# Weight parts interleaved column by column, and a distance table for one product, in a two-layer hybrid block on one core

## The chip, the core and the metric

The kernel runs on one core of one Trainium2 chip. The time is device microseconds of one execution. Three runs of the kernel before are shown, and one profiled execution, from which all rows come.

## The reference

The reference takes 256 tokens of width 1024, puts 16 learned tokens ahead of them, and applies two layers. A layer is a mixer and a feed-forward block, each behind a root-mean-square norm, and each added to its input. The mixer multiplies by one wide matrix and splits the result into the inputs of three branches (retention, a gated recurrence in chunks, differential attention) and three gates; each branch is multiplied by a matrix of its own, the gated sum by an output matrix. The feed-forward block is:

```python
u = jnp.where(valid[None, :, None], hn @ w_ffn_in, 0.0)
up = jnp.pad(u, ((0, 0), (CONV_W - 1, 0), (0, 0)))
c = conv_b + sum(conv_w[j] * up[:, j:j + l] for j in range(CONV_W))
gate, val = jnp.split(c, 2, axis=-1)
return (jax.nn.silu(gate) * val) @ w_ffn_out
```

A last norm ends it. Everything is float32. What matters here is that nearly all of the work is products of a long stream of weights with an activation `x` of at most 272 tokens.

## The kernel before

**Layout.** Features lie on the 128 partitions and tokens along the free axis, 272 of them (16 + 256). An activation of width 1024 is eight slices of 128 features, `x_k`, each 272 columns of 4 bytes. Tiles of four such slices stand next to each other, so a slice begins 1088 bytes after the one ahead of it: 64 bytes further on, counted modulo 256.

**Three products for one.** A float32 product is made of three products in a rounded float32 format (`fp32r` in the profile). Both sides are split into a high part and a low part: `hi` is the value rounded, `lo` is the rest. For each weight tile of 128x128 TensorE does high times high (L910), high weight times low `x` (L911) and low weight times high `x` (L912), all into one PSUM tile `main`. The weight tile is what is loaded into the array (LDWEIGHTS), `x` is what streams through it. Each of the three matmuls has a load of its own, which the trace shows in the lane PEld, beside the matmul that runs ahead of it.

**The stream of weights.** The weights are stored in the order of use, as 404 chunks of eight tiles (128x1024 float32, 512 KB). For every chunk SP issues the DMA to `wraw` (three buffers), ScalarE copies it with rounding to `whi` (four buffers), VectorE subtracts to give `wlo` (four buffers). Each of these is one instruction for a whole chunk, with very few exceptions; they read `wraw` without gaps and leave gaps in what they write. A product works through its tiles in the order `_turns` gives: a pair of output tiles f = 0, 1 for each input slice k.

**Where a tile lies in its chunk.** `_places` leaves gaps between the tiles, such that the tile for slice k starts at a fixed place modulo 256 bytes (`LINE`), which moves by 64 bytes from k to k + 1 as `x_k` does. The two numbers in `APART` set it, the first where 272 columns stream, the second in most of the second layer, where only 258 do (the streamed columns then start 14 columns, 56 bytes, later, `T0`). `BLOCK` makes up for `x` that lies in other buffers. With the addresses of the built program, a weight tile starts 48 bytes after the start of the columns that stream against it where 272 do, and 48 bytes ahead of it where 258 do, both modulo 256. The fourth pair of the second feed-forward product (`fo`, j = 3) has no wanted place in the first layer, and the whole last product has none in the second layer, where the chunk itself streams (512 columns) and the activations `ghi` and `glo` are loaded (L1513 to L1515).

**Order.** All instructions are recorded by `_Plan` and put into an order by its costs and due times; an engine then works in that order. A chunk's copy and subtraction are due 6 us (`LEAD`) ahead of its matmuls. A product's output is taken out of PSUM by VectorE or ScalarE (`evacuate`, `rotate`), and the branches' small products are spread among the large ones by hand-written marks in `ORDER`.

Of the kernel before, what the change touches and what calls it, by code (L numbers as in the profile page):

```python
# [11 lines left out]
F32 = mybir.dt.float32  # L12
F32R = mybir.dt.float32r
U8 = mybir.dt.uint8
AF = mybir.ActivationFunctionType
ALU = mybir.AluOpType
PSUM = bass.MemoryType.PSUM
ADD, SUB, MUL = ALU.add, ALU.subtract, ALU.mult

P = 128  # L20
DEPTH = 2
# [18 lines left out]
CHUNK_TILES = 8  # L40
# [52 lines left out]
def _turns(li):  # L93

    pairs = [x for x in ORDER if x[0][0] not in MARKS]
    if li == DEPTH - 1:
        pairs = [x for x in pairs if x[0] != "fo"]  # L100
    groups = [[x] for x in pairs]
    if li == 0:
        groups[:2] = [pairs[:2]]
    turned = [[pairs[pairs.index((name, 0)) + DEFER - 1]] for name in ("hq", "fi")]
    out = []
    for group in groups:
        if group == [("fo", 3)]:
            out.append([("fo", 3, k, f) for f in range(2) for k in range(FK)])
        else:
            nk = _ktiles(group[0][0])  # L110
            out.append([x + (k, f) for k in range(nk // 2) for x in group for f in range(2)])
            out[-1] += [x + (k, f) for x in group for k in range(nk // 2, nk) for f in range(2)]
            if group in turned:
                out[-1] = out[-1][nk:] + out[-1][:nk]
    if li == DEPTH - 1:
        out.append([("fo", j, k, f) for k in range(FK) for j in range(KD // 2) for f in range(2)])
    return out
# [2 lines left out]
STREAM = sum(2 * _ktiles(n) for n, _ in ORDER if n[0] not in MARKS)  # L120


LINE = 256
APART = (240, 200)
BLOCK = 64
ROOM = CHUNK_TILES * P + 2 * LINE // 4
T0 = META - 2
FULL = ("rk", "rv", "hf", "hi", "dk", "dv")

# [1 line left out]
def _places(depth=DEPTH):  # L131

    wants = []
    for li in range(depth):
        for name, j, k, _ in sum(_turns(li), []):
            if name == "fo" and (li == DEPTH - 1 or j == 3):
                wants.append(None)
                continue  # L140
            short = li == DEPTH - 1 and name not in FULL
            wants.append(APART[short] + BLOCK * (name[0] == "b" or name in ("wo", "fo")) + 64 * (k % 4))
    out = []
    for c in range(0, len(wants), CHUNK_TILES):
        at, places = 0, []
        for want in wants[c : c + CHUNK_TILES]:
            if want is not None:
                at += (want // 4 - at) % (LINE // 4)
            places.append(at)
            at += P  # L150
        assert at <= ROOM
        out.append(places)
    return out


def _runs(places):


    runs = []
    for i, at in enumerate(places):  # L160
        if runs and at == runs[-1][1] + runs[-1][2] * P:
            runs[-1][2] += 1
        else:
            runs.append([i, at, 1])
    out = []
    for i, at, n in runs:
        if out and out[-1][4] == n and (out[-1][3] == 1 or at == out[-1][1] + out[-1][2] * out[-1][3]):
            if out[-1][3] == 1:
                out[-1][2] = at - out[-1][1]
            out[-1][3] += 1  # L170
        else:
            out.append([i, at, 0, 1, n])
    return out
# [424 lines left out]
class _Weights:  # L598
# [3 lines left out]
    def __init__(self, plan, pool, w, act, dve, sp):  # L602
        self.plan, self.pool, self.w = plan, pool, w
        self.act, self.dve, self.sp = act, dve, sp
        self.used = 0
        self.places = _places()

    def part(self, t, at, step, runs, n):

        return bass.AP(t.tensor, t.offset + at, [list(t.ap[0]), [max(step, 1), runs], [1, n * P]])  # L610

    def next(self):
        c, i = divmod(self.used, CHUNK_TILES)
        self.used += 1
        if i == 0:
            due = self.plan.key
            room = [P, ROOM]
            raw = self.plan.tile(self.pool, [P, CHUNK_TILES * P], F32, "wraw", 3, f"wraw{c}")
            hi = self.plan.tile(self.pool, room, F32R, "whi", 4, f"whi{c}")
            lo = self.plan.tile(self.pool, room, F32R, "wlo", 4, f"wlo{c}")  # L620
            self.plan.key = due - LEAD
            pieces = 1 if c > 1 else 2
            for p in range(pieces):
                n = CHUNK_TILES // pieces
                cols = slice(p * n * P, (p + 1) * n * P)
                self.sp.dma_start(raw[:, cols], self.w[c][:, cols])
                for first, at, step, runs, each in _runs(self.places[c][p * n : (p + 1) * n]):
                    src = raw[:, (p * n + first) * P : (p * n + first + runs * each) * P].rearrange("p (r x) -> p r x", r=runs)
                    self.act.activation(self.part(hi, at, step, runs, each), src, AF.Copy)
                    self.dve.tensor_tensor(out=self.part(lo, at, step, runs, each), in0=src, in1=self.part(hi, at, step, runs, each).bitcast(F32), op=SUB)  # L630
            self.plan.key = due
            self.cut = hi, lo
        hi, lo = self.cut
        at = self.places[c][i]
        return hi[:, at : at + P], lo[:, at : at + P]

    def chunk(self):

        for _ in range(CHUNK_TILES):
            self.next()  # L640
        return self.cut


def build(tc, a, depth=DEPTH, probe=None):
# [1073 lines left out]
```

## Time and profile before

| | |
|---|---|
| median of 3 runs | 1304.37 us (1304.02 to 1306.12) |
| profiled execution, own time | 1304.55 us |
| span in its trace | 1302.8 us |
| TensorE busy | 1293.8 us, 99% of the span |
| VectorE busy | 990.1 us, 76% |
| ScalarE busy | 853.1 us, 65% |
| GpSimd busy | 85.0 us, 7% |
| DMA | 219.01 MB, mean 168 GB/s |
| granted TensorE clock | full in all 40 slices |

Busy time says that an engine has an instruction under way. Matmuls overlap in the array, so a matmul's own duration (285 ns or so) is not what it costs: the cost is the distance from its start to the next one's start. That is read from how many matmuls a stretch of time holds. In such a count the two records that only reach into the stretch at its ends are taken off.

### The profile page before, as it was taken

What the parts mean: (1) busy time and instruction counts of PE and PEld (TensorE: products, weight loads), DVE (VectorE), ACT (ScalarE), POOL (GpSimd) and SP (SyncE); (2) the same over time, 40 slices, a digit from 0 to 9 for tenths busy, and PEclk for the clock granted to TensorE, in tenths of its full rate; (3) what the DMA queues carried; (4) which work ended last, traced back from release to release, by engine and by line L of the source; (5) the groups of instructions that cost most, each with busy time, mean ns of one, the idle gap of its engine ahead of it and who ended that gap; (6) DMA issues with size and microseconds to landing.
All of it is one profiled execution on the core that took longest, in us unless ns stands there. A gap on an engine that the chain in (4) does not pass through costs nothing.

```text
span 1302.8 us, 27243 instructions
## 1 busy us (share of the span) xinstructions
PE 1293.8 (99%) x10970; PEld 1271.2 (98%) x10970; DVE 990.1 (76%) x1738; ACT 853.1 (65%) x1486; POOL 85.0 (7%) x162
## 2 busy tenths in 40 slices
PE   9999999999999999999999999999999999999998
PEld 8999999999999999999999999999999999999986
DVE  7685888698686789886564868886987868998753
ACT  6765565767677577776456664657666876777743
POOL 4000000000100020000030000000011100200000
PEclk9999999999999999999999999999999999999999
DMA  8655545444544545555555555454446456566653
GB/s 277 196 161 152 169 150 157 139 138 155 162 143 155 184 163 183 179 178 172 175 180 172 161 170 172 144 168 145 140 136 194 147 162 197 161 206 191 203 181 110
DMA packets 60751, 219.01 MB, mean 168 GB/s; under 512 B 6864, under 2 KB 6992, under 8 KB 60624
## 3 DMA queue, kind: packets, MB, share of 16 engines
q1 hardware_dynamic: 60336, 216.74, 52.7%
q8 instruction: 86, 1.41, 0.4%
q10 hardware_dynamic: 288, 0.52, 0.1%
q14 instruction: 41, 0.34, 0.1%
HBM read 216.19 MB, written 1.05 MB: 167 GB/s over the span
## 4 chain that ended last, share of the span: by engine, by line
PE 96%; DVE 3%; issue 1%; ACT 0%; DMA 0%; SPq 0%; POOL 0%; DVEq 0%
PE main L910 28%; PE main L912 28%; PE main L911 28%; PE fo L1513 2%; PE fo L1515 2%; PE fo L1514 2%; PE ds L1376 1%; PE do L593 1%; PE ho L593 1%; PE vt L593 1%; PE ro L593 1%; PE ms L593 1%; DVE wlo L593 1%; PE wt L593 0%; PE lev L1099 0%
## 5 line engine op out<-in xcount | busy, mean ns | idle before, releaser
L910 PE MATMUL main<-xh,whi 128*128 128x272 f32 (+1 forms) x2368 | 687.0, 290 | 0.6 <-ACT whi L593 0.6
L912 PE MATMUL main<-xh,wlo 128*128 128x272 f32 (+1 forms) x2368 | 674.7, 285 | 0.5 <-DVE wlo L593 0.4
L911 PE MATMUL main<-xl,whi 128*128 128x272 f32 (+1 forms) x2368 | 674.4, 285 | 0.0
L593 DVE TENSOR_TENSOR wlo<-wraw,whi 128x1024 fp32r<-128x1024 f32 (+1 forms) x408 | 498.2, 1226 | 202.4 <-ACT whi L593 198.2
L593 ACT ACTIVATE whi<-wraw 128x1024 fp32r<-128x1024 f32 (+1 forms) x408 | 426.9, 1049 | 206.6 <-PE main L911 125.6
L910 PEld LDWEIGHTS main<-xh,whi 128*128 128x128 f32 x2368 | 445.1, 188 | 2.2 <-ACT whi L593 0.7
L911 PEld LDWEIGHTS main<-xl,whi 128*128 128x128 f32 x2368 | 446.1, 188 | 0.5
L912 PEld LDWEIGHTS main<-xh,wlo 128*128 128x128 f32 x2368 | 445.1, 188 | 1.4 <-DVE wlo L593 1.4
L593 DVE SCALAR_TENSOR_TENSOR two_b<-u,small,two_b 128x256 f32<-128x256 f32 (+2 forms) x176 | 81.3, 503 | 0.2
L593 POOL TENSOR_TENSOR y<-h,rstd 128x272 f32<-128x272 f32 x32 | 36.5, 1177 | 301.0 <-ACT rstd L593 301.0
L593 ACT ACTIVATE two_b<-u,small 128x272 f32<-128x272 f32 (+1 forms) x88 | 50.1, 598 | 3.1 <-DVE glo L593 1.7
L910 PE MATMUL main<-ghi,whi 128*128 128x272 f32 x176 | 51.0, 290 | 0.0
L912 PE MATMUL main<-ghi,wlo 128*128 128x272 f32 x176 | 50.8, 289 | 0.0
L911 PE MATMUL main<-glo,whi 128*128 128x272 f32 x176 | 50.6, 287 | 0.0
L593 ACT ACTIVATE u<-main 128x544 f32<-128x544 f32 (+1 forms) x36 | 22.1, 613 | 32.5 <-PE main L912 32.5
L910 PE MATMUL main<-b0hi,whi 128*128 128x272 f32 (+1 forms) x128 | 37.7, 295 | 0.0
L910 PE MATMUL main<-b1hi,whi 128*128 128x272 f32 (+1 forms) x128 | 37.4, 292 | 0.0
L912 PE MATMUL main<-b0hi,wlo 128*128 128x272 f32 (+1 forms) x128 | 36.4, 284 | 0.0
L911 PE MATMUL main<-b0lo,whi 128*128 128x272 f32 (+1 forms) x128 | 36.4, 284 | 0.0
L911 PE MATMUL main<-b2lo,whi 128*128 128x272 f32 (+1 forms) x128 | 36.4, 284 | 0.0
L912 PE MATMUL main<-b1hi,wlo 128*128 128x272 f32 (+1 forms) x128 | 36.3, 284 | 0.0
L911 PE MATMUL main<-ylo,whi 128*128 128x272 f32 (+1 forms) x128 | 36.3, 284 | 0.0
(266 smaller groups left out, 1948.0 us busy)
## 6 DMA issues: line engine op xcount, KB each, us to landing
wraw<-in_w SPq DMA_DIRECT2D x402, 512.0 KB, 3.6
h<-in_h SPq DMA_DIRECT2D x4, 272.0 KB, 5.5
dec<-in_dec SPq DMA_DIRECT2D x2, 544.0 KB, 4.6
wraw<-in_w SPq DMA_DIRECT2D x4, 256.0 KB, 4.6
const<-in_const SPq DMA_DIRECT2D x1, 937.0 KB, 7.2
gain<-in_gl SPq DMA_DIRECT2D x1, 512.0 KB, 4.7
out<-y ACTq DMA_DIRECT2D x2, 256.0 KB, 2.7
out<-y SPq DMA_DIRECT2D x2, 256.0 KB, 2.7
```

What stands on the lines that cost most here:

```text
L593: self.plan.add(self.name, lambda: f(*args, **kw), cost, outs, ins, args[2] if method == "activation" else None, count)
L910: nc.tensor.matmul(o, wh, hi, start=first, stop=False)
L911: nc.tensor.matmul(o, wh, lo, start=False, stop=False)
L912: nc.tensor.matmul(o, wl, hi, start=False, stop=last)
L1376: nc.tensor.matmul(ss[m][:, at : at + nk], q[half, hd, q0 : q0 + P], k[half, hd, :nk], start=True, stop=True)
L1513: nc.tensor.matmul(o, gh, wh, start=False, stop=False)
L1514: nc.tensor.matmul(o, gl, wh, start=False, stop=False)
L1515: nc.tensor.matmul(o, gh, wl, start=False, stop=end)
```

## The change

The tiles `whi` and `wlo` of a chunk become one tile `wboth` (four buffers). Column c of the high part lies at element 2c and column c of the low part at element 2c + 1, so that from column to column there are 8 bytes (`WIDE`) instead of 4, for the loads of TensorE, for the writes of ScalarE and VectorE, and for VectorE's reading of the high part. A tile of 128 columns spans 1024 bytes instead of 512.

The places are chosen anew. `APART` becomes (128, 128), and in the sense used above a weight tile now starts 128 bytes after the columns that stream against it, in both layers. The 22 pairs of the first feed-forward product (`fi`) get a distance each from the table `FI`: 0 to 240 in steps of 16, then 8, 40, 72, 104, 136 and 200; the same table is used in both layers. The pair `fo`, j = 3 of the first layer gets a place like the other pairs. The chunks of the last product stay without gaps and without interleaving: 1024 columns of the high part, and 1024 of the low part further on in the same tile.

```diff
@@ -120,35 +120,45 @@
 STREAM = sum(2 * _ktiles(n) for n, _ in ORDER if n[0] not in MARKS)
 
 
+
 LINE = 256
-APART = (240, 200)
+WIDE = 8
+APART = (128, 128)
 BLOCK = 64
-ROOM = CHUNK_TILES * P + 2 * LINE // 4
+ROOM = CHUNK_TILES * P + 3 * LINE // WIDE
+
+FI = tuple(range(0, 256, 16)) + (8, 40, 72, 104, 136, 200)
 T0 = META - 2
 FULL = ("rk", "rv", "hf", "hi", "dk", "dv")
 
 
 def _places(depth=DEPTH):
+
 
 
 
     wants = []
     for li in range(depth):
         for name, j, k, _ in sum(_turns(li), []):
-            if name == "fo" and (li == DEPTH - 1 or j == 3):
+            if name == "fo" and li == DEPTH - 1:
                 wants.append(None)
                 continue
             short = li == DEPTH - 1 and name not in FULL
-            wants.append(APART[short] + BLOCK * (name[0] == "b" or name in ("wo", "fo")) + 64 * (k % 4))
+            apart = FI[j] if name == "fi" else APART[short]
+            apart += LINE - 64 + 4 * T0 * short
+            wants.append(apart + BLOCK * (name[0] == "b" or name in ("wo", "fo")) + 64 * (k % 4))
     out = []
     for c in range(0, len(wants), CHUNK_TILES):
+        mine = wants[c : c + CHUNK_TILES]
+        if None in mine:
+            out.append(None)
+            continue
         at, places = 0, []
-        for want in wants[c : c + CHUNK_TILES]:
-            if want is not None:
-                at += (want // 4 - at) % (LINE // 4)
+        for want in mine:
+            at += (want // WIDE - at) % (LINE // WIDE)
             places.append(at)
             at += P
-        assert at <= ROOM
+        assert at <= ROOM, (at, ROOM)
         out.append(places)
     return out
 
@@ -605,40 +615,44 @@
         self.used = 0
         self.places = _places()
 
-    def part(self, t, at, step, runs, n):
-
-        return bass.AP(t.tensor, t.offset + at, [list(t.ap[0]), [max(step, 1), runs], [1, n * P]])
+    def part(self, t, low, at, step, runs, n):
+
+        return bass.AP(t.tensor, t.offset + 2 * at + low, [list(t.ap[0]), [max(2 * step, 1), runs], [2, n * P]])
 
     def next(self):
         c, i = divmod(self.used, CHUNK_TILES)
         self.used += 1
         if i == 0:
             due = self.plan.key
-            room = [P, ROOM]
             raw = self.plan.tile(self.pool, [P, CHUNK_TILES * P], F32, "wraw", 3, f"wraw{c}")
-            hi = self.plan.tile(self.pool, room, F32R, "whi", 4, f"whi{c}")
-            lo = self.plan.tile(self.pool, room, F32R, "wlo", 4, f"wlo{c}")
+            both = self.plan.tile(self.pool, [P, 2 * ROOM], F32R, "wboth", 4, f"wboth{c}")
             self.plan.key = due - LEAD
             pieces = 1 if c > 1 else 2
             for p in range(pieces):
                 n = CHUNK_TILES // pieces
                 cols = slice(p * n * P, (p + 1) * n * P)
                 self.sp.dma_start(raw[:, cols], self.w[c][:, cols])
-                for first, at, step, runs, each in _runs(self.places[c][p * n : (p + 1) * n]):
-                    src = raw[:, (p * n + first) * P : (p * n + first + runs * each) * P].rearrange("p (r x) -> p r x", r=runs)
-                    self.act.activation(self.part(hi, at, step, runs, each), src, AF.Copy)
-                    self.dve.tensor_tensor(out=self.part(lo, at, step, runs, each), in0=src, in1=self.part(hi, at, step, runs, each).bitcast(F32), op=SUB)
+                if self.places[c] is None:
+                    hi, lo = both[:, cols], both[:, ROOM:][:, cols]
+                    self.act.activation(hi, raw[:, cols], AF.Copy)
+                    self.dve.tensor_tensor(out=lo, in0=raw[:, cols], in1=hi.bitcast(F32), op=SUB)
+                    continue
+                for first, *runs in _runs(self.places[c][p * n : (p + 1) * n]):
+                    src = raw[:, (p * n + first) * P : (p * n + first + runs[2] * runs[3]) * P].rearrange("p (r x) -> p r x", r=runs[2])
+                    hi, lo = (self.part(both, low, *runs) for low in range(2))
+                    self.act.activation(hi, src, AF.Copy)
+                    self.dve.tensor_tensor(out=lo, in0=src, in1=hi.bitcast(F32), op=SUB)
             self.plan.key = due
-            self.cut = hi, lo
-        hi, lo = self.cut
-        at = self.places[c][i]
-        return hi[:, at : at + P], lo[:, at : at + P]
+            self.cut = both
+        if self.places[c] is None:
+            return self.cut[:, : CHUNK_TILES * P], self.cut[:, ROOM : ROOM + CHUNK_TILES * P]
+        return tuple(self.part(self.cut, low, self.places[c][i], 1, 1, 1)[:, 0] for low in range(2))
 
     def chunk(self):
 
         for _ in range(CHUNK_TILES):
-            self.next()
-        return self.cut
+            both = self.next()
+        return both
 
 
 def build(tc, a, depth=DEPTH, probe=None):
```

No instruction changes its place among those of its engine, but for one spot. A row names the tile that is written, the tiles that are read, and the shape of the output. These are ScalarE's rows at the end of the first layer, where the chunks of `fo`, j = 3 are split (`two_c` is a square for the next norm, `xh` its input); first of before, then of the changed kernel:

```order
L593 ACTIVATE whi_1217<-wraw_1216 128x4x256
L593 ACTIVATE whi_1220<-wraw_1219 128x256
L593 ACTIVATE whi_1220<-wraw_1219 128x768
L593 ACTIVATE whi_1226<-wraw_1225 128x1024
L593 ACTIVATE whi_1229<-wraw_1228 128x1024
L593 ACTIVATE whi_1232<-wraw_1231 128x1024
```

```order
L603 ACTIVATE wboth_1022<-wraw_1021 128x4x256
L603 ACTIVATE wboth_1024<-wraw_1023 128x2x256
L603 ACTIVATE wboth_1024<-wraw_1023 128x4x128
L603 ACTIVATE wboth_1029<-wraw_1028 128x8x128
L603 ACTIVATE wboth_1031<-wraw_1030 128x8x128
L603 ACTIVATE wboth_1033<-wraw_1032 128x2x128
L603 ACTIVATE wboth_1033<-wraw_1032 128x6x128
```

The last chunk shown takes two instructions where it took one, since its tiles no longer stand at equal steps; VectorE has the same extra one. The second place is VectorE near the start, with what each row waits for (DMA is a landing in `wraw`, PE a matmul, Activation the copy of the high part); before, then changed:

```order
L593 TENSOR_TENSOR wlo_125<-wraw_123,whi_124 128x4x256 [waits DMAHW2_49,Activation_49]
L593 TENSOR_TENSOR wlo_130<-wraw_128,whi_129 128x4x256 [waits DMAHW3_49,PE_49,Activation_49]
L593 TENSOR_TENSOR sum_102<-sum_102 128x272 [waits Pool_49]
L593 TENSOR_TENSOR wlo_133<-wraw_131,whi_132 128x4x256 [waits DMAHW4_49,PE_49,Activation_49]
```

```order
L603 TENSOR_TENSOR wboth_121<-wraw_120,wboth_121 128x4x256 [waits DMAHW2_49,Activation_49]
L603 TENSOR_TENSOR wboth_125<-wraw_124,wboth_125 128x4x256 [waits DMAHW3_49,Activation_49]
L603 TENSOR_TENSOR sum_102<-sum_102 128x272 [waits Pool_49]
L603 TENSOR_TENSOR wboth_127<-wraw_126,wboth_127 128x4x256 [waits DMAHW4_49,PE_49,Activation_49]
```

At about 170 chunks VectorE no longer waits for TensorE itself: both parts are one buffer now, and ScalarE, whose result VectorE needs anyway, has waited for its last reader.

## The prediction

> **What bounds the kernel now.** I read the page first: the engines, and the chain that ended last.
>
> ```profile
> span 1302.8 us, 27243 instructions
> PE 1293.8 (99%) x10970; PEld 1271.2 (98%) x10970; DVE 990.1 (76%) x1738; ACT 853.1 (65%) x1486; POOL 85.0 (7%) x162
> PE 96%; DVE 3%; issue 1%; ACT 0%; DMA 0%; SPq 0%; POOL 0%; DVEq 0%
> ```
>
> TensorE is never out of work, and the chain runs along it. So the time is the number of matmuls times the distance from one start to the next, and the change can only move it through that distance, unless another engine falls behind. Next come the groups by form, for the counts.
>
> ```profile
> L910 PE MATMUL main<-xh,whi 128*128 128x272 f32 x1536 | 449.6, 293 | 0.6 <-ACT whi L593 0.6
> L912 PE MATMUL main<-xh,wlo 128*128 128x272 f32 x1536 | 441.2, 287 | 0.5 <-DVE wlo L593 0.4
> L910 PE MATMUL main<-xh,whi 128*128 128x258 f32 x832 | 237.5, 285 | 0.0
> L910 PE MATMUL main<-ghi,whi 128*128 128x272 f32 x176 | 51.0, 290 | 0.0
> L910 PE MATMUL main<-b0hi,whi 128*128 128x272 f32 x64 | 19.0, 297 | 0.0
> L910 PE MATMUL main<-b0hi,whi 128*128 128x258 f32 x64 | 18.7, 293 | 0.0
> ```
>
> L910 runs once per weight tile, L911 and L912 as often. b1, b2 and y have the counts of b0. With 272 columns that is 3 x (1536 + 176 + 4 x 64) = 5904 matmuls, with 258 columns 3 x (832 + 4 x 64) = 3264. The idle time ahead of L912, 0.5 us in all, says that the low parts are in time. Then four stretches that hold one kind of matmul, as windows.
>
> ```profile
> core 0: us, PE busy (x) PEld busy (x) DVE busy (x) ACT busy (x) POOL busy (x), PEclk, DMA share, GB/s
> 471.00:640.00 169.00, 169.00 (x1358) 168.92 (x1357) 132.72 (x210) 116.39 (x183) 8.77 (x8) 1.00 0.56 176
> 678.40:699.80 21.40, 21.40 (x170) 21.40 (x169) 12.68 (x15) 13.22 (x15) 0.23 (x2) 1.00 0.60 182
> 1119.00:1230.00 111.00, 111.00 (x943) 111.00 (x942) 99.19 (x169) 85.22 (x143) 5.54 (x6) 1.00 0.62 191
> 1236.50:1296.50 60.00, 60.00 (x262) 48.81 (x260) 27.51 (x29) 26.35 (x34) 0.00 (x0) 1.00 0.47 148
> ```
>
> The reader is to see the distances: 169.00 / 1356 = 124.6 ns with 272 columns in the first layer, 21.40 / 168 = 127.4 in a stretch of the second with the same shape, 111.00 / 941 = 118.0 with 258 columns, 60.00 / 260 = 230.8 with 512. The clock is 1.00 in all. Between 272 and 512 columns a column costs (230.8 - 124.6) / 240 = 0.443 ns. That leaves 124.6 - 272 x 0.443 = 4.1 ns of a matmul (3.7 with 258 columns) that is not paid by the column. And the same shape costs 2.8 ns more in one stretch than in another, at full clock and with no wait: something inside TensorE's own reading delays it. The two readers that run at once are the streaming columns and the load of the next tile.
>
> **Speeds of the two readers.** A load of 128 columns and one of 32, from the groups:
>
> ```profile
> L912 PEld LDWEIGHTS main<-xh,wlo 128*128 128x128 f32 x2368 | 445.1, 188 | 1.4 <-DVE wlo L593 1.4
> L1099 PEld LDWEIGHTS lev<-extra,hf 128*32 128x32 f32 x256 | 3.8, 110 | 0.6 <-issue 0.2
> ```
>
> (188 - 110) / 96 = 0.81 ns per loaded column, 104 ns for a tile. Streaming moves on by 4 bytes in 0.443 ns, 9.0 bytes per ns. Loading moves on by 4 bytes in 0.81 ns, 4.9 bytes per ns; after the change by 8 bytes, 9.9 bytes per ns. So today the stream overtakes the load: in 104 ns it gains some 430 bytes, nearly twice the 256 that the places are counted by. Afterwards the two keep their distance to within 10%, which in 104 ns is some 90 bytes. If what delays is the passing of one reader by the other, most of it goes, and the distance of 128 bytes decides the rest.
>
> **The change part by part.**
>
> Loads of 8-byte steps: no load of the trace has a step, so the price is bounded from both sides. On the good side the part that is not paid by the column goes whole: 5904 x 4.1 ns = 24.2 us and 3264 x 3.7 ns = 12.1 us, together 36 us. On the bad side it doubles, since a load touches twice as many bytes: 36 us more. I take the good end, because the two readers at nearly one speed are nearest to a stream alone, and take off for what follows.
>
> The table for the first feed-forward product: 22 pairs of 16 tiles and three matmuls make 1056 matmuls in each layer, 2112 of the 9168, at 22 distances. Some must be bad ones. I let half of the pairs gain nothing: 528 x (4.1 + 3.7) ns = 4 us in all given back (the other bound: they cost what the worse stretch shows, 2.8 ns on 1056 matmuls, 3 us more).
>
> The last product keeps contiguous chunks and loads: 0. Its chunk is one tile instead of two, and its matmuls have no new wait.
>
> ScalarE and VectorE write with 8-byte steps, and VectorE reads the high part so. Rows:
>
> ```profile
> L593 DVE TENSOR_TENSOR wlo<-wraw,whi 128x1024 fp32r<-128x1024 f32 x400 | 491.9, 1235 | 199.4 <-ACT whi L593 195.2 <-PE wt L593 1.5 <-PE lev L1099 0.7
> L593 DVE TENSOR_TENSOR hf<-hf,he 128x544 f32<-128x544 f32 x4 | 2.9, 719 | 0.0
> L593 DVE TENSOR_TENSOR h<-h,main 128x544 f32<-128x544 f32 x7 | 5.1, 722 | 8.4 <-PE main L912 8.4
> L593 ACT ACTIVATE whi<-wraw 128x1024 fp32r<-128x1024 f32 x400 | 422.0, 1057 | 204.4 <-PE main L911 123.7 <-DMA wraw<-in_w 28.7 <-PE fo L1514 26.6
> L593 ACT ACTIVATE extra<-hq 128x512 f32<-128x512 f32 x4 | 2.7, 668 | 0.0
> L593 ACT ACTIVATE whi<-wraw 128x512 fp32r<-128x512 f32 x6 | 3.7, 621 | 0.3 <-DMA wraw<-in_w 0.3
> ```
>
> The product into `hf` reads and writes every second element, 719 ns; `h` is contiguous, 722. So VectorE pays nothing. `extra` is read at every second element, 668 ns, against 621 of the plain copy of that size. A step on the output is not in the trace for ScalarE; between 0 and 2 x 47 = 94 ns per chunk, so up to 400 x 0.094 = 38 us on an engine that is idle for 450 us. All of that lies beside TensorE. The cover: in the tightest stretch, 1119 to 1230, ScalarE has 85.2 of 111 us and VectorE 99.2. With 258 columns at 114.3 ns that stretch would last 107.6 us, and VectorE would be at 92%. A little less cover, and it holds; if the distance fell to 110 ns it would be 96%, and VectorE's lateness would come next.
>
> Waits: ScalarE's write of a chunk now waits for L912 of four chunks ago, not for L911, one matmul or 0.12 us later. Behind it in ScalarE's queue stand the evacuations of `main` that TensorE needs. The waits show what room there is.
>
> ```profile
> DVE wlo L593 <- ACT whi L593: 198.2, 180, 4.8
> ACT whi L593 <- PE main L911: 125.6, 99, 3.9
> ```
>
> 99 waits x 0.12 us = 12 us of ScalarE, out of its 450 idle; VectorE follows it, and TensorE takes the chunk some microseconds later. I price it at 0, with 1 us as the bound if a few of these reach TensorE. The waits of VectorE on TensorE that fall away were already met when ScalarE had finished. The extra instruction on ScalarE and VectorE, and the two chunks of `fo`, j = 3 that are written in pieces, are under 1 us beside TensorE's work. SP's issues, their order and their sizes stay.
>
> The sum: 1304.55 (span 1302.8, and 1.75 around it) - 36 + 4 = 1272 with the distances as argued. The median of the runs is 0.2 us lower. What I have fitted as the price of a column may itself hold delay by the load, since the load runs beside nearly all 272 columns; two stretches of one shape differ by 2.8 ns. I allow 4 us for that and forecast **1268 us**.
>
> **The rivals.**
>
> *All delay goes.* The column price of 0.443 ns holds delay by the load too. For it: the stretch at 678 us shows that one shape has more than one price. Against it: 512 columns go on for long after the load is over, and still cost it. If the lost part of 272 columns is twice what I fitted, 72 us go, and VectorE's 96% keeps some of it: 1232 to 1250. [...]
>
> *The two readers do not meet at all.* Then step and distance do nothing, and the time stays: 1304 us. For it: TensorE's distances are very even over whole layers. Against it: 127.4 against 124.6 for one shape with nothing waiting. [...]
>
> *The readers keep a bad distance (the other side).* Two readers at one speed that meet once go on meeting for the whole load. The load also starts at an unknown moment of the stream: 14 ns of shift is 128 bytes, so that the chosen 128 may be the bad one. It decides when the distance rises above 124.6 and 118.0 ns in the pairs outside the table. Price: from 127.4 - 124.6 = 2.8 ns on 9168 matmuls, 26 us, to the doubled 36 us and, if the column part is hit likewise, 72 us. 1330 to 1376, with 1340 the likeliest.
>
> *The load becomes the bound.* 104 ns of loading stand under 118.0 ns. If an 8-byte step makes a load 20% slower, it is 125 ns: 258 columns lose 7 ns, 23 us, 272 columns stay: 1327; at 40% slower, 146 ns, it is 9168 x 21 to 28 ns, over 1500. [...]
>
> **How the numbers follow.** My forecast (1250 to 1300) gets 0.40, all delay gone 0.17, no change 0.07, the bad distance 0.27, the load as the bound 0.09. From no change a measurement of this kernel can tell about 0.2%, 2.6 us. Faster by more is 0.57, the same 0.07, slower 0.36. The likeliest case's own range is 1250 to 1300. To leave out no more than 2 in 10, the range for all goes from 1230 to 1350: above it lie the worse third of the bad distances and the slow loads, below it a little of the second case.
>
> **What the profile after would show.** Right: stretches of 272 columns at 119 to 121 ns and of 258 at 113 to 116, the loads' 188 ns unchanged, VectorE's 1235 ns unchanged, ScalarE's 1057 at most 1150. In the first feed-forward product the distance from start to start differs from pair to pair, in the same way in both layers. Wrong: 124 and 118 ns as before (no meeting), over 127 outside the table (a bad distance), a load well over 188 ns, or TensorE idle ahead of L910 and L912 by more than their 1 us (VectorE or ScalarE late).

## The result: slower by 1.2%, and the profile after

| | before | after |
|---|---|---|
| median | 1305.24 us (1304.02 to 1306.58, 4 runs) | 1320.49 us (1320.15 to 1320.87, 4 runs) |
| ratio | | 1.0115, 95% interval 1.0102 to 1.0128 |
| span in the trace | 1302.8 us | 1318.6 us |

The page of the kernel after: its span, its engines, and the chain that ended last.

```profile
span 1318.6 us, 27245 instructions
PE 1310.6 (99%) x10970; PEld 1288.5 (98%) x10970; DVE 991.5 (75%) x1739; ACT 889.0 (67%) x1487; POOL 85.9 (7%) x162
PE 97%; DVE 2%; issue 0%; DMA 0%; ACT 0%; SPq 0%; POOL 0%; DVEq 0%
```

TensorE is as full as before and has the same 10970 matmuls. So the 15.8 us lie in the distance from start to start. The windows of the kernel after show it (two of the stretches of the prediction; the one with 512 columns, moved by 16 us as it comes later; and two that the experiments use, one with 272 columns, one with 258).

```profile
core 0: us, PE busy (x) PEld busy (x) DVE busy (x) ACT busy (x) POOL busy (x), PEclk, DMA share, GB/s
471.00:640.00 169.00, 169.00 (x1341) 168.93 (x1340) 133.25 (x210) 121.79 (x184) 8.80 (x8) 1.00 0.57 175
1119.00:1230.00 111.00, 111.00 (x917) 110.93 (x916) 96.24 (x160) 87.15 (x137) 8.71 (x8) 1.00 0.60 183
1252.50:1312.50 60.00, 60.00 (x261) 48.55 (x259) 27.70 (x30) 26.10 (x33) 0.00 (x0) 1.00 0.47 148
520.00:620.00 100.00, 100.00 (x795) 100.00 (x795) 76.59 (x126) 74.14 (x112) 0.00 (x0) 1.00 0.57 175
1080.00:1110.00 30.00, 30.00 (x249) 30.00 (x249) 21.19 (x26) 18.25 (x20) 0.00 (x0) 1.00 0.55 171
```

With 272 columns 169.00 / 1339 = 126.2 ns (124.6 before), with 258 columns 111.00 / 915 = 121.3 (118.0), with 512 columns 60.00 / 259 = 231.7 (230.8, which is one matmul more in the count, and no difference). The last two rows give 126.1 and 121.5. The same two stretches of the kernel before:

```profile
520.00:620.00 100.00, 100.00 (x804) 100.00 (x803) 76.46 (x125) 70.22 (x110) 0.00 (x0) 1.00 0.57 175
1080.00:1110.00 30.00, 30.00 (x256) 30.00 (x255) 23.46 (x29) 16.96 (x23) 0.00 (x0) 1.00 0.64 193
```

These are 124.7 and 118.1 ns. One matmul more or less moves the first by 0.2 ns and the second by 0.5. Then the groups of the kernel after, with the three loads and the two engines that write the weights.

```profile
L925 PEld LDWEIGHTS main<-xl,wboth 128*128 128x128 f32 x2368 | 467.0, 197 | 0.4
L926 PEld LDWEIGHTS main<-xh,wboth 128*128 128x128 f32 x2368 | 464.6, 196 | 1.3 <-DVE wboth L603 1.3
L603 DVE TENSOR_TENSOR wboth<-wraw,wboth 128x1024 fp32r<-128x1024 f32 x399 | 491.2, 1236 | 217.1 <-ACT wboth L603 215.8
L603 ACT ACTIVATE wboth<-wraw 128x1024 fp32r<-128x1024 f32 x399 | 459.2, 1154 | 205.6 <-PE main L926 124.0 <-PE fo L1529 27.1 <-DMA wraw<-in_w 26.1
```

A load takes 196 to 197 ns in place of 188. ScalarE pays 97 ns a chunk, VectorE 1 ns. TensorE hardly waits for either: of the waits of its `main` on them only this is left.

```profile
PE main L926 <- DVE wboth L603: 0.4, 2, 0.2
```

### The profile page after: what moved, and what is told of

It reads as the page before. It is cut to its first block, busy times and chain, and to the rows that moved or that the text cites. A ratio compares the mean times of both kernels' runs of the same rounds, so it can differ in the third digit from the quotient of the medians.

```text
span 1318.6 us, 27245 instructions
## 1 busy us (share of the span) xinstructions
PE 1310.6 (99%) x10970; PEld 1288.5 (98%) x10970; DVE 991.5 (75%) x1739; ACT 889.0 (67%) x1487; POOL 85.9 (7%) x162
## 4 chain that ended last, share of the span: by engine, by line
PE 97%; DVE 2%; issue 0%; DMA 0%; ACT 0%; SPq 0%; POOL 0%; DVEq 0%
PE main L924 29%; PE main L926 28%; PE main L925 28%; PE fo L1528 2%; PE fo L1527 2%; PE fo L1529 2%; PE ds L1390 1%; PE do L603 1%; PE ho L603 1%; PE ro L603 1%; PE vt L603 1%; PE ms L603 1%; PE lev L1113 1%; PE wt L603 0%; DMA h<-in_h 0%
## 5 line engine op out<-in xcount | busy, mean ns | idle before, releaser
L924 PE MATMUL main<-xh,wboth 128*128 128x272 f32 (+1 forms) x2368 | 693.2, 293 | 0.1
L926 PE MATMUL main<-xh,wboth 128*128 128x272 f32 (+1 forms) x2368 | 681.0, 288 | 0.5 <-DVE wboth L603 0.4
L925 PE MATMUL main<-xl,wboth 128*128 128x272 f32 (+1 forms) x2368 | 679.2, 287 | 0.0
L603 DVE TENSOR_TENSOR wboth<-wraw,wboth 128x1024 fp32r<-128x1024 f32 (+2 forms) x409 | 498.7, 1225 | 221.0 <-ACT wboth L603 219.7
L603 ACT ACTIVATE wboth<-wraw 128x1024 fp32r<-128x1024 f32 (+2 forms) x409 | 465.7, 1142 | 209.4 <-PE main L926 127.8
L925 PEld LDWEIGHTS main<-xl,wboth 128*128 128x128 f32 x2368 | 467.0, 197 | 0.4
L924 PEld LDWEIGHTS main<-xh,wboth 128*128 128x128 f32 x2368 | 465.6, 197 | 1.7 <-ACT wboth L603 0.3
L926 PEld LDWEIGHTS main<-xh,wboth 128*128 128x128 f32 x2368 | 464.6, 196 | 1.3 <-DVE wboth L603 1.3
L924 PE MATMUL main<-ghi,wboth 128*128 128x272 f32 x176 | 51.0, 290 | 0.0
L926 PE MATMUL main<-ghi,wboth 128*128 128x272 f32 x176 | 50.9, 289 | 0.0
L925 PE MATMUL main<-glo,wboth 128*128 128x272 f32 x176 | 50.7, 288 | 0.0
L924 PE MATMUL main<-b0hi,wboth 128*128 128x272 f32 (+1 forms) x128 | 38.1, 298 | 0.0
L924 PE MATMUL main<-b1hi,wboth 128*128 128x272 f32 (+1 forms) x128 | 37.8, 295 | 0.0
L926 PE MATMUL main<-b0hi,wboth 128*128 128x272 f32 (+1 forms) x128 | 36.6, 286 | 0.0
```

What stands on the lines that cost most here:

```text
L603: self.plan.add(self.name, lambda: f(*args, **kw), cost, outs, ins, args[2] if method == "activation" else None, count)
L924: nc.tensor.matmul(o, wh, hi, start=first, stop=False)
L925: nc.tensor.matmul(o, wh, lo, start=False, stop=False)
L926: nc.tensor.matmul(o, wl, hi, start=False, stop=last)
```

## The experiments

My first theory (S) was that the step of 8 bytes from column to column alone makes the load dearer and that the places do nothing; the rival (P) was that the step is harmless and 128 bytes a bad place.

**Undoing one half of the change at a time.** The first run keeps the weights as they were before and takes only the new places (the pair `fo`, j = 3 stays without one):

```diff
 # the kernel before, with
-APART = (240, 200)
+APART = (128, 128)
+FI = tuple(range(0, 256, 16)) + (8, 40, 72, 104, 136, 200)
...
-            wants.append(APART[short] + ...
+            apart = FI[j] if name == "fi" else APART[short]
+            apart += LINE - 64 + 4 * T0 * short
+            wants.append(apart + ...
```

> The first kernel's weights (high and low parts apart, 4 bytes from column to column), with the changed kernel's distances from x (128 everywhere, the table of 22 for the first feed-forward product). Theory S (the 8-byte step makes the load itself dearer: 188 to 197 ns): loads back at 188 ns, 124.6 to 125.5 ns from start to start with 272 columns and 118 to 119 with 258, total 1304 to 1310 us. Rival P (the distance 128 is a bad one, the step is harmless): loads at 197 ns or the distances at 126 and 121 all the same, total 1317 to 1322 us. Half and half, 1312, would say that each carries a part.

The second keeps the step of 8 bytes and takes the old places back:

```diff
 # the kernel after, with
-APART = (128, 128)
+APART = (48, 208)
...
-            apart = FI[j] if name == "fi" else APART[short]
+            apart = APART[short]
```

> The changed kernel's interleaved weights, 8 bytes from column to column, with the first kernel's distances (48 and 208 bytes within the line, no table for the first feed-forward product). Theory S (the step): loads at 197 ns, 126 and 121 to 122 ns from start to start, total 1317 to 1323 us. Rival P (the distance): loads near 188 ns, 124.6 and 118.0 ns, total 1303 to 1307 us or below.

The new places alone took 1323.76 us (ratio 1.014, 1.0125 to 1.0156), the step alone 1315.54 us (1.0074, 1.0062 to 1.0087), with the kernel before at 1306.20 beside them. Both expectations failed: either half alone is slower, and the places alone are slower than the whole change (the two intervals, 1.0125 to 1.0156 and 1.0102 to 1.0128, just touch, but the distances with 258 columns below say the same). The windows of the new places with the old step:

```profile
520.00:620.00 100.00, 100.00 (x798) 100.00 (x797) 77.00 (x127) 70.48 (x111) 0.00 (x0) 1.00 0.55 176
1080.00:1110.00 30.00, 30.00 (x239) 30.00 (x238) 19.97 (x23) 16.49 (x17) 0.00 (x0) 1.00 0.55 175
```

And of the new step at the old places:

```profile
520.00:620.00 100.00, 100.00 (x804) 100.00 (x803) 77.44 (x126) 72.86 (x110) 0.00 (x0) 1.00 0.55 177
1080.00:1110.00 30.00, 30.00 (x248) 30.00 (x248) 23.22 (x29) 18.23 (x22) 0.00 (x0) 1.00 0.58 187
```

With 272 columns the places cost (100 / 796 = 125.6 ns) and the step does not (100 / 802 = 124.7). With 258 columns both do, 30 / 237 = 126.6 and 30 / 246 = 122.0. The means over all matmuls, taken from their start times in each trace (distances of 150 ns and more, where something else comes between, are left out), separate the two halves, and the places at 128 bytes ("at 128") from the other places of the table ("table"):

| step, places | 272 columns | 258 columns |
|---|---|---|
| 4 bytes, old (before) | 124.8 | 118.2 |
| 4 bytes, new: at 128 / table | 125.9 / 125.7 | 123.9 / 119.7 |
| 8 bytes, old | 124.9 | 121.6 |
| 8 bytes, new: at 128 / table (after) | 125.9 / 126.3 | 121.3 / 121.0 |

By the table of means this adds up. The step at the old places: 3264 x 3.4 + 5904 x 0.1 = 11.7 us, and the span grew by 1313.7 - 1302.8 = 10.9. The places with the new step: 5904 x 1.0 or a little more, less 3264 x 0.4, about 5 us, and the span grew by 1318.6 - 1313.7 = 4.9. Together this is the whole difference, to within the 3 us over which spans of one kernel scatter (the kernel before beside these two runs had 1302.1 to 1305.4 us). With 4 bytes the places at 128 cost 258 columns most, 5.7 ns; with 8 bytes nothing more, as if something else already held the distance up there.

The start times of the first run show more, pair by pair of the table. With 272 columns the pair at 48 bytes is the fastest of the 22 (124.2 ns, the others up to 126.8), with 258 columns the pair at 208 bytes (118.1 ns, the others 119.0 to 126.2, and the slowest is the one at 128). These are the places of the kernel before, and there these two pairs take the same 124.2 and 118.1 ns. So the old places were already the best of the 22 that the table tries on this product.

The equal means of 272 columns, 124.8 and 124.9 ns for the step at the old places, hide two opposite effects. Cut the 5904 matmuls, in their order, into 123 groups of 48. In the trace of the kernel before, 19 of the groups (912 matmuls) stand at 126.1 to 128.1 ns, 127.4 in the mean, and the rest at 124.4. The stretch of 127.4 ns that the prediction showed lies in four of them. With the new step at the old places the same 19 stand at 124.9, and the rest at 124.9 too. The prediction's stretch in that run:

```profile
678.40:699.80 21.40, 21.40 (x174) 21.40 (x174) 12.77 (x17) 14.27 (x16) 1.25 (x5) 1.00 0.53 174
```

That is 21.40 / 172 = 124.4 ns for 127.4. The step thus took 2.5 ns from 912 matmuls, 2.3 us, and put 0.5 ns on the other 4992, 2.4 us. The theory that the rest tests (F): with the longer step the load itself becomes the longer of the two with 258 columns, and the places disturb only where a load takes nearly the whole distance.

**The price of the load by itself.** All matmuls but the first of an output stream 128 columns, which is meant to make the load of the next tile longer than the stream, so that it sets the distance. What the other columns would add is left out of the sums. Each is an edit on its own kernel, so the second has the new places too.

```diff
+                m = o.shape[-1] if first else 128
-                nc.tensor.matmul(o, wh, hi, start=first, stop=False)
-                nc.tensor.matmul(o, wh, lo, start=False, stop=False)
-                nc.tensor.matmul(o, wl, hi, start=False, stop=last)
+                nc.tensor.matmul(o[:, :m], wh, hi[:, :m], start=first, stop=False)
+                nc.tensor.matmul(o[:, :128], wh, lo[:, :128], start=False, stop=False)
+                nc.tensor.matmul(o[:, :128], wl, hi[:, :128], start=False, stop=last)
```

> The first kernel; in its products with 272 and 258 columns only the first matmul of an output streams all columns, all others stream 128 (the rest of the sum is left out), so that the load of 128 columns is longer than the stream and sets the distance. All theories: 104 to 108 ns from start to start (128 columns at 0.81 ns a column, with little on top). Loads about 188 ns or shorter, as they wait less.

> The changed kernel with the same columns left out. Theory S (a load with 8 bytes from column to column is dearer by itself): 113 to 121 ns from start to start, 8 to 14 ns above the first kernel's narrow form. Rival P (only the place against x matters) and rival M (only the meeting with a stream of x of equal pace matters): 104 to 108 ns, as in the first kernel's narrow form.

A window of each, at full clock, the kernel before first, the kernel after in the second fence.

```profile
500.00:580.00 80.00, 79.86 (x712) 79.69 (x711) 76.38 (x133) 65.30 (x108) 0.00 (x0) 1.00 0.63 201
```

```profile
500.00:580.00 80.00, 80.00 (x675) 79.93 (x674) 73.38 (x119) 63.74 (x101) 8.46 (x8) 1.00 0.57 184
```

79.86 / 710 = 112.5 ns and 80.00 / 673 = 118.9 ns, with a few full first matmuls in both. So with a short stream the matmuls follow each other at 112 ns and not at the 104 to 108 that I expected of the first, and with 8 bytes from column to column at 6 ns more. I take this for the time of the load. The load's rows were longer here (199 and 208 ns), where I had expected no longer ones: rows of 199 ns that follow each other at 112.5 ns do not tell what a load takes by itself.

**The load as a floor.** The same edit with 240 columns in place of 128, the second with the new step at the old places.

> The first kernel with 240 columns streamed in all matmuls but the first of an output (the other columns are left out). By the column price, 118.0 less 18 x 0.443 = 110.0 ns; the load's floor of the narrow run is 112 (median). Theory F (the distance is the longer of stream and load): 111 to 113 ns. Rival A (load and stream add up in part, whatever their lengths): 110 ns or less.

> The 8-byte step at the first kernel's distances with 240 columns streamed in the same matmuls. Theory F (a floor of 119 ns by the load, which 258 columns already touch): 119 to 121 ns, hardly below the 121.6 of 258 columns. Rival T (the step slows the stream, by 3.4 ns whatever the load): 121.6 less 8, 113 to 114 ns.

One stretch of the first layer's shape and one of the second's, the old step:

```profile
480.00:600.00 120.00, 120.00 (x1070) 120.00 (x1070) 98.59 (x154) 86.88 (x135) 0.00 (x0) 1.00 0.63 203
1050.00:1080.00 30.00, 30.00 (x268) 30.00 (x268) 29.83 (x51) 23.88 (x41) 6.25 (x6) 1.00 0.52 165
```

And the new step:

```profile
480.00:600.00 120.00, 120.00 (x1016) 120.00 (x1016) 99.99 (x164) 91.90 (x140) 0.00 (x0) 1.00 0.61 193
1090.00:1120.00 30.00, 30.00 (x251) 30.00 (x250) 29.31 (x50) 24.82 (x41) 5.50 (x6) 1.00 0.53 167
```

With the old step 112.4 and 112.8 ns, with the new one, at the same places, 118.3 and 120.5. That is what 128 columns took (112.5 and 118.9), to within 1.6 ns, so it is not the stream that sets these distances. That the 112 ns of the old step are the load, and no other fixed pace, no run with a short load under a short stream shows. In the second layer's places, 18 columns fewer than 258 save 118.1 - 112.8 = 5.3 ns with 4 bytes and 122.0 - 120.5 = 1.5 ns with 8. So with 8 bytes the 258 columns, at 122.0, stand within a few ns of that floor, and 272 columns, at 124.7, are clear of it. By this reading the step costs the 258 columns and hardly the 272. The rival, that the step slows the stream itself by 3.4 ns whatever the load, would have given 113 to 114 ns for 240 columns. What makes 122.0 ns out of a floor of 118.9 and a stream of 118.1 is not shown: the longer of the two alone would be 118.9.

**Half the load.** All but the first and the last matmul of an output load 64 weight columns, so that half of the output's rows are not summed; the streams are whole.

```diff
+                m, z = (P if first else 64), (P if last else 64)
+                nc.tensor.matmul(o[:m], wh[:, :m], hi, start=first, stop=False)
+                nc.tensor.matmul(o[:64], wh[:, :64], lo, start=False, stop=False)
+                nc.tensor.matmul(o[:z], wl[:, :z], hi, start=False, stop=last)
```

> The first kernel; in its products only the first and the last matmul of an output load 128 weight columns, all others 64 (half of the rows of the output are not summed). [...] Theory C (a price of each matmul that no load changes): 124 to 125 and 118 ns as before. [...]

> The changed kernel with the same halved loads. Theory S (a whole load at 8 bytes from column to column, 119 ns by the narrow run, reaches the stream with 258 columns): a half load of about 60 ns is far below the stream, so the loss of 3 ns with 258 columns goes: within 1 ns of the first kernel's halved form with 258 columns and with 272. Rival T (the step disturbs the stream of x as such, by the lines that it touches): 1.5 to 3 ns above the first kernel's halved form with 258 columns.

> 4 bytes from column to column, the changed kernel's distances, half loads (half of the output's rows are not summed). Theory M2 (what the distance costs is a meeting of load and stream, so it goes with a shorter load): the dearer 125.9 ns with 272 columns back to 124.3 to 124.8, the dearer 123.9 with 258 columns at distance 128 back to 117.8 to 118.5. Rival X (x or its place alone is what costs): 125.9 and 123.9 as with whole loads.

The windows, first of the kernel before, then of the kernel after, then of the old step at the new places, all with half loads.

```profile
520.00:620.00 100.00, 100.00 (x803) 100.00 (x802) 76.57 (x125) 70.18 (x110) 0.00 (x0) 1.00 0.55 175
1080.00:1110.00 30.00, 30.00 (x257) 30.00 (x256) 24.39 (x31) 18.59 (x26) 0.00 (x0) 1.00 0.65 196
```

```profile
520.00:620.00 100.00, 100.00 (x803) 100.00 (x802) 76.56 (x123) 72.08 (x109) 0.00 (x0) 1.00 0.55 178
1080.00:1110.00 30.00, 30.00 (x255) 29.87 (x253) 23.38 (x30) 17.66 (x24) 0.00 (x0) 1.00 0.62 205
```

```profile
520.00:620.00 100.00, 100.00 (x805) 100.00 (x804) 76.46 (x126) 70.47 (x110) 0.00 (x0) 1.00 0.55 175
1080.00:1110.00 30.00, 30.00 (x254) 30.00 (x253) 23.52 (x30) 17.07 (x23) 0.00 (x0) 1.00 0.61 192
```

| half loads | 272 columns | 258 columns |
|---|---|---|
| 4 bytes, old places | 124.8 | 117.8 |
| 8 bytes, new: at 128 / table | 124.3 / 125.1 | 117.9 / 119.3 |
| 4 bytes, new: at 128 / table | 124.5 / 124.7 | 119.3 / 118.4 |

The first row is the one that decides the prediction. Half of the load is gone, and 272 columns take 124.8 ns as before, 258 columns 117.8 for 118.2. The few ns that are not paid by the column do not come from the length of the load (theory C). A fixed price of each load would look the same; no run is without loads.

The mean again hides two parts. The 19 slow groups of the kernel before fall from 127.4 to 124.8 ns, and the rest rises from 124.4 to 124.8, for which I have no reason. The prediction's stretch with half loads, 21.40 / 171 = 125.1 ns:

```profile
678.40:699.80 21.40, 21.40 (x173) 21.40 (x172) 13.16 (x15) 13.21 (x15) 0.39 (x3) 1.00 0.57 189
```

The other two rows: what the step and the places cost goes for the most part when the load gets shorter, 123.9 to 119.3 and 121.3 to 117.9 with 258 columns, 125.9 to 124.3 and 124.5 with 272. On the table's places 1 ns or so stays. So the load can disturb the stream; in the kernel before it did so in about one matmul of ten, 912 of 9168, by some 2.6 ns. Why in these groups and not in their neighbours, no run tells.

**Interleaving or step, and a longer step.** High and low parts 8 bytes from column to column in places of their own, and then 16 bytes from column to column; both at the old places, with two buffers for four.

```diff
 # the new step at the old places, with (parts apart)
-        return bass.AP(t.tensor, t.offset + 2 * at + low, ...
+        return bass.AP(t.tensor, t.offset + 2 * at + low * 2 * ROOM, ...
 # or with (16 bytes)
-WIDE = 8
+WIDE = 16
-        return bass.AP(t.tensor, t.offset + 2 * at + low, [list(t.ap[0]), [max(2 * step, 1), runs], [2, n * P]])
+        return bass.AP(t.tensor, t.offset + 4 * at + low, [list(t.ap[0]), [max(4 * step, 1), runs], [4, n * P]])
 # and in both
-            both = self.plan.tile(self.pool, [P, 2 * ROOM], F32R, "wboth", 4, f"wboth{c}")
+            both = self.plan.tile(self.pool, [P, 4 * ROOM], F32R, "wboth", 2, f"wboth{c}")
```

> High and low parts 8 bytes from column to column, but each in a place of its own with holes between (not interleaved), with the first kernel's distances; two buffers of weights in place of four, as four don't fit, so the total may carry waits for buffers, and the windows tell. Theory S (the step alone makes the load dearer): loads 196 to 197 ns, 121 to 122 ns with 258 columns and 124.5 to 125 with 272, as with interleaving. Rival I (interleaving, high beside low in a line, is what costs): loads 188 ns, 118 ns with 258 columns.

> 16 bytes from column to column (high part, low part, two empty places), the first kernel's distances, two buffers of weights. Theory S1 (the load pays for the bytes it runs over: 7 ns for the 512 bytes more from 4 to 8 bytes by the narrow runs, 112 to 119): 14 ns more for 1024 bytes more, a load of 133 ns sets the distance everywhere: 133 ns with 258 and 272 columns, LDWEIGHTS rows near 205 to 215 ns. [...] Rival N (no more than at 8 bytes): 197 ns rows, 121 to 125 ns.

Parts apart, a load's group and the wait that two buffers bring (the total was 1378.54 us, and isn't used):

```profile
L925 PEld LDWEIGHTS main<-xl,wboth 128*128 128x128 f32 x2368 | 467.0, 197 | 0.4
```

```profile
PE main L926 <- DVE wboth L603: 20.9, 37, 1.4
```

The load takes 197 ns as with interleaving, and the means are 124.9 and 121.7 ns, as with interleaving at the same places (124.9 and 121.6). It is the step that costs, not the low part beside the high one. With 16 bytes, a load's group and a window:

```profile
L925 PEld LDWEIGHTS main<-xl,wboth 128*128 128x128 f32 x2368 | 782.7, 331 | 0.0
```

```profile
900.00:930.00 30.00, 30.00 (x130) 30.00 (x130) 15.65 (x19) 16.48 (x20) 0.00 (x0) 1.00 0.29 98
```

30.00 / 128 = 234 ns from start to start, a little over twice the distance of the first kernel with short streams (2 x 112.5), and 2345.72 us in all. The price of a step is thus not one of bytes run over, by which S1 had 133 ns, and not the same at 16 bytes as at 8 (N, 121 to 125): from 4 to 8 bytes the distance rises by 6% (112.5 to 118.9 ns), from 8 to 16 it doubles (118.9 to 234). Why the one step costs so little and the other so much, no run tells.

**The table taken out.** One edit on the kernel after: `apart = APART[short]` for all pairs.

> The changed kernel with its table for the first feed-forward product taken out: these pairs stand at 128 like the rest. From the changed kernel's trace, 258 columns take 121.0 ns on the table's places and 121.3 at 128, 272 columns 126.2 and 125.9. Theory S (with the 8-byte step the place within the line hardly matters): 1319 to 1322 us, no change. The prediction's own step (the table gives 4 us back): 1324 to 1325 us. With 4 bytes the table gave 123.9 less 119.6 ns on 1056 matmuls of 258 columns, 4.5 us.

1320.10 us (1.0115, 1.0098 to 1.0132), the same as with the table.

## Why the prediction was wrong

I forecast 1268 us, faster; it was 1320.49, slower. That lies within the range for all cases, 1230 to 1350, but on the side to which I had given 0.36.

*TensorE's distance alone sets the time:* right. ScalarE's 97 ns a chunk (I had 0 to 94), VectorE's 1 ns, and the waits on both (0.4 us) cost next to nothing; the last product's distance stayed.

*The part of a matmul that is not paid by the column goes, 36 us:* this is the step that failed. I took 4.1 and 3.7 ns as delay by the passing of the two readers, from an intercept and from one stretch that was 2.8 ns slower. With half of the load gone they were still there, 124.8 and 117.8 ns. With half loads the span is 1300.0 us at the old step and places and 1298.9 at the new step and places, against 1302.3 of the kernel before beside them: 2 to 3 us is what even that brings. With it fall the 4 us that I allowed for delay inside the column price. The stretch at 678 us was rightly read: its 2.8 ns were delay by the load, and half loads and the new step both removed it (125.1 and 124.4 ns). My error was to take it as a sign for all 9168 matmuls. Only 912 had such a delay, about 2.4 us in all, and the step puts as much on the other 272-column matmuls and 11 us on those of 258 columns. What the 4.1 and 3.7 ns are paid for stays open.

*A load's duration, "188 ns unchanged":* wrong, 197 ns, and more to the point 118.9 for 112.5 ns from start to start with short streams. I read 104 ns from two LDWEIGHTS rows, and so saw 14 ns of room below 118.0; by the short streams there were 118.0 - 112.5 = 5.5, and the step, 6.4 ns, took them all.

*The table gives back 4 us of the gain:* nothing with 8 bytes, 1320.10 us without it and 1320.49 with it, both at 1.0115 of the kernel before. (What I wrote ahead of the last run has this step with the wrong sign: by the prediction the kernel without its table would have been 4 us faster, not slower.) From pair to pair of the table its means go from 120.2 to 122.4 ns with 258 columns and from 124.8 to 127.5 with 272, but not in the same way in both layers as I had said: the pairs at 48 bytes are the best of one layer (124.8) and average in the other (121.4).

*The rivals.* All delay goes, 1232 to 1250 us: no run that streams all columns came near, not even with half loads (1301.79 and 1300.64 us). No meeting at all: true of nine tenths of the kernel before, by the half loads, not of its 912 slow matmuls, nor of the other versions. A bad distance: it is there, 1.0 ns on 272 columns instead of the 2.8 or more that I gave it, 5 us. The load as the bound, my last rival at 0.09: it is the larger part. Its shape was right (258 columns lose, 272 do not), its size 3.4 ns for my 7, 11 us for 23.

## What to carry to other kernels

Before pricing a collision as removable, take one of the two parties away (half the load, or a narrow stream) and see whether the distance moves; an intercept from two shapes is not a delay. Go stretch by stretch in this, since a mean that stays may hide a part that gained and a part that lost. The room of a load behind a stream is to be measured with a short stream and not taken from the duration of its rows: here 5.5 ns for the 14 that the rows gave. And two harmful edits need not add: with 258 columns the places at 128 cost 5.7 ns with 4 bytes from column to column (118.2 to 123.9) and nothing with 8 (121.6 and 121.3), so each half is run alone.

No version that computes the whole sum beat the kernel before, and even with half loads the means stayed at 124.3 ns or more with 272 columns and at 117.8 or more with 258, against its 124.8 and 118.2. By the spans with half loads (1300.0 and 1298.9 us against 1302.3) places and steps have, as an estimate, some 2 to 3 us left to give here, most of it in the 912 slow matmuls (912 x 2.6 ns).

## What was not expected of the hardware

- Matmuls that each load 128 columns, with float32 values 4 and 8 bytes apart, followed each other at 112.5 and 118.9 ns with streams of 128 columns, and with values 16 bytes apart at 234 ns with streams of 272, all at full clock.
- Half a load left the mean distance of 272 columns where it was (124.8 ns), so the 4.1 ns that the prediction's 0.443 ns a column leaves of a matmul, an estimate, did not come from the length of the load.
- In 912 of 5904 such matmuls the load did delay the stream, 127.4 ns for 124.4 in the others, and half a load or an 8-byte step took that away (124.8 and 124.9).
- The place of the weights within 256 bytes moved a matmul by up to 5.7 ns in the mean (118.2 to 123.9, 258 columns, 4 bytes), where the distance with short streams is 112.5, and by 1.5 ns with half the load (117.8 to 119.3). Why 128 bytes is bad there and 208 is not, no run tells.
